# Attention scores in high and low float32r parts, with the rotated dimensions of both key segments stacked on 128 rows

## The chip, the cores and the metric

The kernel runs on one core of a Trainium2 chip. The metric is the device time of one execution in microseconds (us); the kernel before took 1618.8 us, the median of three runs (1617.66 to 1621.54). One more execution was taken with the profiler, and all rows of the trace come from it.

## The reference

The reference is a trunk of four layers on a latent sequence of 256 tokens and a context of 256 tokens, model width 1024: a gated spatial mixer (SGU), an RWKV-7 layer with a scan in both directions, a latent attention layer (MLA), and a second SGU. Only the third is touched. It projects the input to a query latent of rank 768, a key and value latent of rank 256, one shared key of 64 dimensions that is to be rotated, and gates. From the latents come 16 heads: queries of 128 unrotated ("nope") and 64 rotated ("rope") dimensions, keys of 128 nope dimensions that take the shared 64 behind them, and values of 128. Queries and keys are normalised over their 192 dimensions. Cut to what matters:

```
q_rot, k_rot = apply_rope(q, cos, sin), apply_rope(k, cos, sin)   # rotates the last 64 of 192
s = concat([q @ k_ctx.T, q_rot @ k_rot.T])                        # 256 context + 256 latent keys
p = softmax(s * 192 ** -0.5)
o = p[:, :256] @ v_ctx + p[:, 256:] @ v
x = x + gate * ((o * silu(z)) @ w_out)
```

So a query meets the context keys unrotated and the latent keys rotated.

## The kernel before, in words

All activations lie with features on the 128 partitions and tokens along the columns: 512 columns, first the context, then the latent segment (`X` is the slice of the latter). Large products are made from pieces in the type float32r: a value is cut into a high part, rounded to float32r, and a low part, the rest; hi*hi + hi*lo + lo*hi stands for the product. `split` makes both parts, the high one as a copy on ScalarE (ACT), the low one as a subtraction on VectorE (DVE). `mm3` issues the products, `wload` brings a weight tile by a DMA from SyncE's (SP's) queue and splits it (lines 178, 183, 184), with `raw`, `hi` and `lo` buffers in rings. `phase` sets the sizes of these rings: the MLA layer has four `raw` tiles of 1024 columns and three of `hi` and `lo`.

`mla` first makes the latents and the shared key `kr` (its 64 rows stand twice, on rows 0 to 63 and 64 to 127). Then 16 steps of gates (`gates`) run interleaved with `latents` and with the projection of the first pair of heads. After it comes a loop over eight pairs `g`: `attend(g)` and `project(g + 1)` are interleaved, and from `g` = 5 on some blocks of the output projection too.

`project` makes for one pair: two heads' nope keys (`keys`: product, copy, square, sum with the shared key's squares), values (`values`), and in `scaled` the key's norm `r` over 192 dimensions, the scaled nope key (L1207) and the scaled rope key, 64 rows a head, both heads in one tile `krh` (L1208). Then the rope queries of both heads together (`qo`, one head on each half of the rows), their rotated copy (`rotate`: a product with a matrix that swaps the halves of 32 with a sign on TensorE (PE), two multiplications with cosine and sine and an addition on DVE), and the nope queries (`queries`), with their norms (`norms`, which go into the softmax's scale).

`attend` makes a score block of 128 queries of one head against 512 keys in one bank of PSUM, by three products in plain float32: nope over 512 columns (L1304), unrotated rope over the 256 context columns on 64 rows (L1305), rotated rope over the 256 latent columns on 64 rows (L1306). Row maximum on DVE (L1308), exponential with a row sum on ACT (L1311), division on DVE (L1313). `weighted` transposes the block on PE, multiplies with the values, applies the gate and splits the result for the output projection; it runs one head late.

The order is set by a planner at build time: it takes the instructions in order of the program's interleaving, lets ready ones go ahead on a simulated clock, and gives each engine a fixed queue. A tile's buffers (the last number in `tl(tag, shape, bufs)`) are released when its last reader is done. On the chip each engine runs its queue in order and waits on semaphores.

Of the kernel before, what the change touches and what calls it, by code (L numbers as in the profile page):

```python
# [9 lines left out]
F32R = mybir.dt.float32r  # L10
AF = mybir.ActivationFunctionType
ALU = mybir.AluOpType
# [5 lines left out]
T = 512  # L18
# [80 lines left out]
def body(tc, I, out):  # L99
# [70 lines left out]
    def wload(src, n=None):  # L170
        return next(wparts(src, n))
# [896 lines left out]


    def mla(m):  # L1070
        with phase("2", 0, 0, 4, psum=(("pA", 4), ("pB", 4)), wn=1024, hi=3):
            ep = env["a"]

            def tl(tag, shape, bufs, dtype=F32):
# [97 lines left out]
            def rotate(dst, src):  # L1172
                p = ps("sw", "pA")
                PE.matmul(p[:, 0:256], swap, src, start=True, stop=True)
                t = tl("t1", q256, 4)
                V.tensor_tensor(t, p[:, 0:256], rope[:, 1], ALU.mult)
                V.tensor_tensor(dst, src, rope[:, 0], ALU.mult)
                V.tensor_tensor(dst, dst, t, ALU.add)

            def project(g, d):  # L1180

                w = wload(I["ml_kv"][g])
                d["kn"] = []
                kt = lambda: tl("hx" if g else "s", [128, T], 8 if g else 16)
                d["krh"], d["v"] = kt(), []

                def keys(hh):
                    p = ps("kn", "pA")
                    for k in range(2):
                        sl = slice(k * 256 + hh * 128, k * 256 + hh * 128 + 128)  # L1190
                        mm3(p, w[0][:, sl], w[1][:, sl], ckv[k], k == 0, k == 1)
                    t = kt()
                    S.copy(t, p)
                    sq = tl("lt", [128, T], 4)
                    S.activation(sq, t, AF.Square)
                    V.tensor_tensor(sq[0:64], sq[0:64], krs, ALU.add)
                    d["kn"].append(t)
                    return sq

                def scaled(hh, sq):  # L1200
                    p = ps("kss", "pA")
                    PE.matmul(p, ones, sq, start=True, stop=True)
                    hf = slice(64 * hh, 64 * hh + 64)
                    r = tl("lt", [128, T], 4)
                    rsqrt_bc(r, p, 1.0 / 192, eps)
                    t = d["kn"][hh]
                    V.scalar_tensor_tensor(out=t, in0=t, scalar=vec[:, 10:11], in1=r, op0=ALU.mult, op1=ALU.mult)  # L1207
                    V.tensor_tensor(d["krh"][hf], krg[hf], r[hf], ALU.mult)  # L1208

                def values(tb):  # L1210
                    p = ps("pv", "pA")
                    t = tl("v", [128, 2, 256], 4)
                    for b in range(2):
                        pp_ = p[:, b * 256:b * 256 + 256]
                        for k in range(2):
                            sl, ws = slice((tb + b) * 128, (tb + b) * 128 + 128), slice(512 + k * 256, 768 + k * 256)
                            PE.matmul(pp_, ckv[k][:, 0, sl], w[0][:, ws], start=k == 0, stop=False)
                            PE.matmul(pp_, ckv[k][:, 0, sl], w[1][:, ws], start=False, stop=False)
                            PE.matmul(pp_, ckv[k][:, 1, sl], w[0][:, ws], start=False, stop=k == 1)
                        d["v"].append(t[:, b])  # L1220
                    S.copy(t.rearrange("p a b -> p (a b)"), p)

                k0 = keys(0)
                yield
                k1 = keys(1)
                yield
                values(0)
                yield
                scaled(0, k0)
                yield  # L1230
                values(2)
                yield
                scaled(1, k1)
                yield
                qo, ro, qrs = tl("qo", q256, 2), tl("qr", q256, 2), tl("t1", q256, 4)
                mm256(wload(I["ml_qr"][g], 768), cq, qo)
                S.activation(qrs, qo, AF.Square)
                S.activation(qo, qo, AF.Identity, scale=vec[:, 9:10])
                yield
                d["qo"], d["qr"], d["qn"] = qo, ro, []  # L1240
                d["rq"] = rq = tl("rq", [128, 4], 2)

                def queries(hh):
                    hf = slice(64 * hh, 64 * hh + 64)
                    t = tl("qn", q256, 4)
                    mm256(wload(I["ml_qn"][g * 2 + hh], 768), cq, t)
                    sq = tl("t1", q256, 4)
                    S.activation(sq, t, AF.Square)
                    V.tensor_tensor(sq[hf], sq[hf], qrs[hf], ALU.add)
                    S.activation(t, t, AF.Identity, scale=vec[:, 8:9])  # L1250
                    d["qn"].append(t)
                    return sq

                def norms(hh, sq):
                    pq = ps("qss", "pA")
                    for qb in range(2):
                        PE.matmul(pq[:, qb:qb + 1], sq[:, qb * 128:qb * 128 + 128], ones[:, 0:1], start=True, stop=True)
                    rh = rq[:, hh * 2:hh * 2 + 2]
                    S.activation(rh, pq[:, 0:2], AF.Ln, scale=1.0 / 192, bias=eps)
                    S.activation(rh, rh, AF.Exp, scale=-0.5, bias=lsc)  # L1260

                q0 = queries(0)
                yield
                rotate(ro, qo)
                yield
                q1 = queries(1)
                norms(0, q0)
                yield
                yield
                norms(1, q1)  # L1270
                yield
# [22 lines left out]
            def attend(g, d, before):  # L1294

                rq = d["rq"]
                for hh in range(2):
                    hf = slice(64 * hh, 64 * hh + 64)
                    pt = []
                    for qb in range(2):  # L1300
                        qs = slice(qb * 128, qb * 128 + 128)
                        j = hh * 2 + qb
                        p = ps("sc", "pB")
                        PE.matmul(p, d["qn"][hh][:, qs], d["kn"][hh], start=True, stop=False)  # L1304
                        PE.matmul(p[:, 0:256], d["qo"][hf, qs], d["krh"][hf, 0:256], start=False, stop=False)  # L1305
                        PE.matmul(p[:, 256:512], d["qr"][hf, qs], d["krh"][hf, 256:512], start=False, stop=True)  # L1306
                        sm = tl("sm", [128, 4], 4)
                        V.tensor_reduce(out=sm[:, 0:1], in_=p, op=ALU.max, axis=AX.X)  # L1308
                        V.scalar_tensor_tensor(out=sm[:, 1:2], in0=sm[:, 0:1], scalar=-1.0, in1=rq[:, j:j + 1], op0=ALU.mult, op1=ALU.mult)
# [14 lines left out]
            cq = [tl("cq", [128, 2, 256], 6, F32R) for _ in range(6)]  # L1324
            ckv = [tl("ckv", [128, 2, T], 2, F32R) for _ in range(2)]
            krs = tl("krs", [64, T], 1)
            krg = tl("krg", [128, T], 1)

            def latents():
                yield from latent(ckvr, 6, 256, T, ckv)  # L1330
                S.activation(krs, kr[0:64], AF.Square)
                S.activation(krg, kr, AF.Identity, scale=vec[:, 11:12])
                krr = tl("t1", q256, 4)
                rotate(krr, krg[:, X])
                V.tensor_copy(krg[:, X], krr)
                yield
                yield from latent(cqr, 0, 768, 256, cq)

# [66 lines left out]
```

## Time and profile before

| what | value |
|---|---|
| median of three runs | 1618.8 us |
| the profiled execution | 1616.74 us |
| its span, first to last instruction | 1615.0 us |
| mean granted clock of TensorE, share of full | 0.970 |
| attention layer, from the latents to the last score | about 1046 to 1385 us |
| of it the loop over head pairs | about 1152 to 1390 us |
| period of the loop while it is regular | 28.53 us |

Busy times are unions of an engine's instructions, without issuing or waiting. Matmuls are pipelined and their ends are modelled, so the price of a stream of matmuls is read from their starts. In a timeline, brackets behind a row say how long the engine was idle before it and what ended that. PEld is TensorE's loading of weights, which overlaps PE.

### The profile page before, as it was taken

What the parts mean: (1) busy time and instruction counts of PE and PEld (TensorE: products, weight loads), DVE (VectorE), ACT (ScalarE), POOL (GpSimd) and SP (SyncE); (2) the same over time, 40 slices, a digit from 0 to 9 for tenths busy, and PEclk for the clock granted to TensorE, in tenths of its full rate; (3) what the DMA queues carried; (4) which work ended last, traced back from release to release, by engine and by line L of the source; (5) the groups of instructions that cost most, each with busy time, mean ns of one, the idle gap of its engine ahead of it and who ended that gap; (6) DMA issues with size and microseconds to landing.
All of it is one profiled execution on the core that took longest, in us unless ns stands there. A gap on an engine that the chain in (4) does not pass through costs nothing.

```text
span 1615.0 us, 28890 instructions
## 1 busy us (share of the span) xinstructions
PE 1516.5 (94%) x11666; PEld 1173.8 (73%) x11666; DVE 1151.3 (71%) x2101; ACT 788.0 (49%) x1404; POOL 124.8 (8%) x156
## 2 busy tenths in 40 slices
PE   5999999999599998899899899899999999979998
PEld 2787888888467644777676677678777777768887
DVE  3789998845788367586796854778766666665876
ACT  4544231222455353444445333569866766456543
POOL 0000000000500142212303000000000000000000
PEclk8999999999799999799999999999999999989999
DMA  9676658631044553432433133134321232265452
GB/s 366 242 288 232 234 192 305 233 105 52 36 145 167 174 159 77 145 90 80 126 103 87 59 113 103 62 129 137 121 76 47 78 92 92 66 234 196 169 183 79
DMA packets 95174, 229.05 MB, mean 142 GB/s; under 512 B 26048, under 2 KB 52160, under 8 KB 80576
## 3 DMA queue, kind: packets, MB, share of 16 engines
q1 hardware_dynamic: 92736, 223.00, 41.1%
q10 hardware_dynamic: 2304, 4.20, 0.7%
q8 instruction: 92, 1.51, 0.4%
q14 instruction: 42, 0.34, 0.1%
HBM read 208.81 MB, written 17.83 MB: 140 GB/s over the span
## 4 chain that ended last, share of the span: by engine, by line
PE 46%; DVE 6%; ACT 6%; issue 1%; POOL 1%; DMA 0%; ACTq 0%; DVEq 0%; POOLq 0%
PE fm L310 4%; PE op L310 4%; PE pg L904 3%; PE op L975 2%; PE fm L311 2%; PE op L311 2%; PE pz L310 2%; PE pu L310 2%; PE po L1286 2%; PE sc L1304 2%; PE pe L790 2%; PE sc L1305 1%; PE pv L376 1%; PE pz L311 1%; PE pv L377 1%
## 5 line engine op out<-in xcount | busy, mean ns | idle before, releaser
L184 DVE TENSOR_TENSOR lo<-raw,hi 128x2048 fp32r<-128x2048 f32 (+3 forms) x147 | 247.2, 1683 | 105.0 <-ACT hi L183 104.4
L183 ACT CAST hi<-raw 128x2048 fp32r<-128x2048 f32 (+3 forms) x161 | 212.3, 1324 | 218.8 <-PE op L314 40.5
L251 DVE SCALAR_TENSOR_TENSOR junk<-adaw,scb 128x1024 f32<-128x1024 f32 x112 | 136.9, 1222 | 13.6 <-DMA adaw<-in_ada_wT 11.7
L310 PE MATMUL op<-s,hi 128*128 128x512 f32 x256 | 91.6, 400 | 0.0
L375 PE MATMUL pv<-hi,hp 128*128 128x512 f32 x192 | 76.6, 401 | 9.1 <-ACT hi L183 6.0
L376 PE MATMUL pv<-lo,hp 128*128 128x512 f32 x192 | 76.4, 398 | 1.7 <-DVE lo L184 1.7
L310 PE MATMUL fm<-hx,hi 128*128 128x512 f32 x200 | 73.8, 409 | 4.1 <-ACT hx L304 3.8
L377 PE MATMUL pv<-hi,hp 128*128 128x512 f32 x192 | 76.2, 397 | 0.0
L904 PE MATMUL pg<-xz,wz 128*128 128x256 f32 x256 | 71.1, 412 | 0.0
L311 PE MATMUL op<-s,lo 128*128 128x256 f32 x256 | 71.1, 280 | 0.0
L313 PE MATMUL pj<-xs,hi 128*128 128x512 f32 x128 | 53.9, 423 | 12.3 <-ACT xs L304 10.2
L794 DVE TENSOR_TENSOR E<-pe,masks 128x512 f32<-128x512 f32 x64 | 41.6, 683 | 26.6 <-PE pe L790 23.9
L695 POOL TENSOR_TENSOR BK<-f 64x256 f32<-64x256 f32 x64 | 56.5, 882 | 44.3 <-DVE f L688 31.2
L311 PE MATMUL fm<-hx,lo 128*128 128x256 f32 x200 | 56.5, 287 | 2.0 <-DVE lo L184 2.0
L1004 PE MATMUL pv<-wv,xv 128*128 128x512 f32 x128 | 57.3, 596 | 0.0
L310 PEld LDWEIGHTS op<-s,hi 128*128 128x128 f32 x256 | 48.1, 188 | 12.6 <-issue 1.3
L314 PE MATMUL pj<-xs,hi 128*128 128x512 f32 x128 | 52.7, 412 | 4.0 <-DVE xs L305 4.0
L310 PE MATMUL fm<-cq,hi 128*128 128x512 f32 x144 | 55.7, 423 | 0.0
L904 PEld LDWEIGHTS pg<-xz,wz 128*128 128x128 f32 x256 | 47.1, 197 | 11.5 <-issue 3.6
L975 PE MATMUL op<-Y,wo 128*128 128x256 f32 x192 | 53.8, 415 | 1.3 <-DVE xT L979 1.3
L315 PE MATMUL pj<-xs,lo 128*128 128x512 f32 x128 | 52.5, 412 | 2.2 <-DVE lo L184 2.1
L313 PE MATMUL pu<-hp,hi 128*128 128x512 f32 x128 | 50.7, 396 | 0.0
(392 smaller groups left out, 4027.3 us busy)
## 6 DMA issues: line engine op xcount, KB each, us to landing
adaw<-in_ada_wT SPq DMA_DIRECT2D x36, 1024.0 KB, 6.2
raw<-in_sgu_v SPq DMA_DIRECT2D x16, 1024.0 KB, 5.9
raw<-in_sgu_u SPq DMA_DIRECT2D x16, 1024.0 KB, 5.3
raw<-in_sgu_z SPq DMA_DIRECT2D x16, 1024.0 KB, 5.0
raw<-in_sgu_o SPq DMA_DIRECT2D x16, 1024.0 KB, 4.8
adaw<-in_ada_w SPq DMA_DIRECT2D x24, 512.0 KB, 10.2
xz<-xz SPq DMA_DIRECT2D x32, 256.0 KB, 3.9
raw<-in_ml_z SPq DMA_DIRECT2D x16, 512.0 KB, 3.7
```

The lines of the kernel that those rows point to most:

```text
L183: S.copy(hi[:, sl], raw[:, sl])
L184: (nc.gpsimd if parts > 1 and i else V).tensor_tensor(lo[:, sl], raw[:, sl], hi[:, sl], ALU.subtract)
L251: V.scalar_tensor_tensor(out=junk, in0=raw[:, f, :], scalar=1.0, in1=scb[:, c, :], op0=ALU.mult, op1=ALU.mult, accum_out=m[:, t * 2 + f, c ...
L310: PE.matmul(p, whi, x, start=start, stop=False)
L311: PE.matmul(p[:, 0:256], wlo, x[:, 0], start=False, stop=stop)
L313: PE.matmul(p, whi, x[:, 0], start=start, stop=False)
L375: PE.matmul(pv[tb], hs[k][:, 0, sl], whi[:, ws_], start=k == 0, stop=False)
L376: PE.matmul(pv[tb], hs[k][:, 0, sl], wlo[:, ws_], start=False, stop=False)
L377: PE.matmul(pv[tb], hs[k][:, 1, sl], whi[:, ws_], start=False, stop=k == 7)
L904: PE.matmul(p, ws[k // 4][:, k % 4, pr * 128:pr * 128 + 128], xs[k // 2][:, k % 2, :], start=k == 0, stop=k == 7)
L975: PE.matmul(p[:, ob], w[:, k, ob, :], y[:, k], start=k == 0, stop=k == 1)
L1004: PE.matmul(p, xv[:, k, tb * 128:tb * 128 + 128], ws[k // 4][:, k % 4, :], start=k == 0, stop=k == 7)
```

## The change

Four things. (1) The nope keys and nope queries are kept as high and low parts (`kt` tiles in float32r; `qn` with two halves), and a nope score is three float32r products. (2) The rope part of both segments becomes one product over 128 rows: the queries of a head hold the unrotated 64 dimensions on one half of the rows and the rotated ones on the other (`qo`, one column block a head); the keys `krg[hh]` hold the unrotated shared key in the context columns of the first half, the rotated one in the latent columns of the other half, and zeros elsewhere. This product is split too, so a score block is six float32r products of 512 columns. (3) For that, the rope queries are scaled into the two halves by two ACT instructions, copied to the opposite rows by two DMAs on SP's queue (`qx`), rotated from there, and added into place by two 64-row additions; the scaled rope keys are made by a multiplication on GpSimd (POOL) and split by ACT and DVE. (4) `raw` has three buffers, not four; `hx` tiles are taken four a pair, not three; `qo` and `qx` have one buffer each, `qn` three, the stacked and split keys (`rp`) three, the stacked and split queries (`qp`) two.

```diff
@@ -1068,7 +1068,7 @@
 
 
     def mla(m):
-        with phase("2", 0, 0, 4, psum=(("pA", 4), ("pB", 4)), wn=1024, hi=3):
+        with phase("2", 0, 0, 3, psum=(("pA", 4), ("pB", 4)), wn=1024, hi=3):
             ep = env["a"]
 
             def tl(tag, shape, bufs, dtype=F32):
@@ -1174,38 +1174,44 @@
                 PE.matmul(p[:, 0:256], swap, src, start=True, stop=True)
                 t = tl("t1", q256, 4)
                 V.tensor_tensor(t, p[:, 0:256], rope[:, 1], ALU.mult)
-                V.tensor_tensor(dst, src, rope[:, 0], ALU.mult)
-                V.tensor_tensor(dst, dst, t, ALU.add)
+                u = tl("t1", q256, 4)
+                V.tensor_tensor(u, src, rope[:, 0], ALU.mult)
+                for hf, x in dst:
+                    V.tensor_tensor(x, u[hf], t[hf], ALU.add)
 
             def project(g, d):
 
                 w = wload(I["ml_kv"][g])
                 d["kn"] = []
-                kt = lambda: tl("hx" if g else "s", [128, T], 8 if g else 16)
-                d["krh"], d["v"] = kt(), []
+                kt = lambda: tl("hx" if g else "s", [128, T], 8 if g else 16, F32R)
+                d["kr"], d["v"] = [], []
 
                 def keys(hh):
                     p = ps("kn", "pA")
                     for k in range(2):
                         sl = slice(k * 256 + hh * 128, k * 256 + hh * 128 + 128)
                         mm3(p, w[0][:, sl], w[1][:, sl], ckv[k], k == 0, k == 1)
-                    t = kt()
+                    t = tl("kf", [128, T], 2)
                     S.copy(t, p)
                     sq = tl("lt", [128, T], 4)
                     S.activation(sq, t, AF.Square)
                     V.tensor_tensor(sq[0:64], sq[0:64], krs, ALU.add)
-                    d["kn"].append(t)
-                    return sq
-
-                def scaled(hh, sq):
+                    return t, sq
+
+                def scaled(hh, t, sq):
                     p = ps("kss", "pA")
                     PE.matmul(p, ones, sq, start=True, stop=True)
-                    hf = slice(64 * hh, 64 * hh + 64)
                     r = tl("lt", [128, T], 4)
                     rsqrt_bc(r, p, 1.0 / 192, eps)
-                    t = d["kn"][hh]
                     V.scalar_tensor_tensor(out=t, in0=t, scalar=vec[:, 10:11], in1=r, op0=ALU.mult, op1=ALU.mult)
-                    V.tensor_tensor(d["krh"][hf], krg[hf], r[hf], ALU.mult)
+                    x = kt(), kt()
+                    S.copy(x[0], t)
+                    V.tensor_tensor(x[1], t, x[0], ALU.subtract)
+                    d["kn"].append(x)
+                    nc.gpsimd.tensor_tensor(r, krg[hh], r, ALU.mult)
+                    x = tl("rp", [128, 2, T], 3, F32R)
+                    split(r, x)
+                    d["kr"].append(x)
 
                 def values(tb):
                     p = ps("pv", "pA")
@@ -1226,29 +1232,36 @@
                 yield
                 values(0)
                 yield
-                scaled(0, k0)
+                scaled(0, *k0)
                 yield
                 values(2)
                 yield
-                scaled(1, k1)
-                yield
-                qo, ro, qrs = tl("qo", q256, 2), tl("qr", q256, 2), tl("t1", q256, 4)
-                mm256(wload(I["ml_qr"][g], 768), cq, qo)
-                S.activation(qrs, qo, AF.Square)
-                S.activation(qo, qo, AF.Identity, scale=vec[:, 9:10])
-                yield
-                d["qo"], d["qr"], d["qn"] = qo, ro, []
+                scaled(1, *k1)
+                yield
+
+                qo, qx, qrs = tl("qo", [128, 2, 256], 1), tl("qx", q256, 1), tl("t1", q256, 4)
+                qt = tl("t1", q256, 4)
+                mm256(wload(I["ml_qr"][g], 768), cq, qt)
+                S.activation(qrs, qt, AF.Square)
+                for hh in range(2):
+                    hf, of = (slice(64 * i, 64 * i + 64) for i in (hh, 1 - hh))
+                    S.activation(qo[hf, hh], qt[hf], AF.Identity, scale=vec[hf, 9:10])
+                    nc.sync.dma_start(out=qx[of], in_=qo[hf, hh])
+                yield
+                d["qn"] = []
                 d["rq"] = rq = tl("rq", [128, 4], 2)
 
                 def queries(hh):
                     hf = slice(64 * hh, 64 * hh + 64)
-                    t = tl("qn", q256, 4)
+                    t = tl("qf", q256, 2)
                     mm256(wload(I["ml_qn"][g * 2 + hh], 768), cq, t)
                     sq = tl("t1", q256, 4)
                     S.activation(sq, t, AF.Square)
                     V.tensor_tensor(sq[hf], sq[hf], qrs[hf], ALU.add)
-                    S.activation(t, t, AF.Identity, scale=vec[:, 8:9])
-                    d["qn"].append(t)
+                    x = tl("qn", [128, 2, 256], 3, F32R)
+                    S.activation(x[:, 0], t, AF.Identity, scale=vec[:, 8:9])
+                    V.scalar_tensor_tensor(out=x[:, 1], in0=t, scalar=vec[:, 8:9], in1=x[:, 0], op0=ALU.mult, op1=ALU.subtract)
+                    d["qn"].append(x)
                     return sq
 
                 def norms(hh, sq):
@@ -1261,7 +1274,9 @@
 
                 q0 = queries(0)
                 yield
-                rotate(ro, qo)
+                rotate([(slice(64, 128), qo[64:128, 0]), (slice(0, 64), qo[0:64, 1])], qx)
+                d["qr"] = tl("qp", [128, 2, 2, 256], 2, F32R)
+                split(qo, d["qr"])
                 yield
                 q1 = queries(1)
                 norms(0, q0)
@@ -1295,15 +1310,16 @@
 
                 rq = d["rq"]
                 for hh in range(2):
-                    hf = slice(64 * hh, 64 * hh + 64)
                     pt = []
                     for qb in range(2):
                         qs = slice(qb * 128, qb * 128 + 128)
                         j = hh * 2 + qb
                         p = ps("sc", "pB")
-                        PE.matmul(p, d["qn"][hh][:, qs], d["kn"][hh], start=True, stop=False)
-                        PE.matmul(p[:, 0:256], d["qo"][hf, qs], d["krh"][hf, 0:256], start=False, stop=False)
-                        PE.matmul(p[:, 256:512], d["qr"][hf, qs], d["krh"][hf, 256:512], start=False, stop=True)
+                        (kh, kl), q = d["kn"][hh], d["qn"][hh]
+                        PE.matmul(p, q[:, 0, qs], kh, start=True, stop=False)
+                        PE.matmul(p, q[:, 0, qs], kl, start=False, stop=False)
+                        PE.matmul(p, q[:, 1, qs], kh, start=False, stop=False)
+                        mm3(p, d["qr"][:, 0, hh, qs], d["qr"][:, 1, hh, qs], d["kr"][hh], False, True)
                         sm = tl("sm", [128, 4], 4)
                         V.tensor_reduce(out=sm[:, 0:1], in_=p, op=ALU.max, axis=AX.X)
                         V.scalar_tensor_tensor(out=sm[:, 1:2], in0=sm[:, 0:1], scalar=-1.0, in1=rq[:, j:j + 1], op0=ALU.mult, op1=ALU.mult)
@@ -1324,15 +1340,20 @@
             cq = [tl("cq", [128, 2, 256], 6, F32R) for _ in range(6)]
             ckv = [tl("ckv", [128, 2, T], 2, F32R) for _ in range(2)]
             krs = tl("krs", [64, T], 1)
-            krg = tl("krg", [128, T], 1)
+
+
+            krg = [tl(f"krg{hh}", [128, T], 1) for hh in range(2)]
 
             def latents():
                 yield from latent(ckvr, 6, 256, T, ckv)
                 S.activation(krs, kr[0:64], AF.Square)
-                S.activation(krg, kr, AF.Identity, scale=vec[:, 11:12])
-                krr = tl("t1", q256, 4)
-                rotate(krr, krg[:, X])
-                V.tensor_copy(krg[:, X], krr)
+                S.activation(kr, kr, AF.Identity, scale=vec[:, 11:12])
+                for hh in range(2):
+                    hf, of = (slice(64 * i, 64 * i + 64) for i in (hh, 1 - hh))
+                    nc.gpsimd.memset(krg[hh][hf, X], 0.0)
+                    nc.gpsimd.memset(krg[hh][of, 0:256], 0.0)
+                    S.copy(krg[hh][hf, 0:256], kr[hf, 0:256])
+                rotate([(slice(64, 128), krg[0][64:128, X]), (slice(0, 64), krg[1][0:64, X])], kr[:, X])
                 yield
                 yield from latent(cqr, 0, 768, 256, cq)
 
```

## Rows read from the trace of the kernel before

**Rows 1.** The page: busy us (share of the span) and instructions of each engine
```profile
PE 1516.5 (94%) x11666; PEld 1173.8 (73%) x11666; DVE 1151.3 (71%) x2101; ACT 788.0 (49%) x1404; POOL 124.8 (8%) x156
```

**Rows 2.** Busy by window: length, PE, PEld, DVE, ACT, POOL, granted clock, DMA
```profile
1092.00:1152.00 60.00, 58.29 (x326) 49.53 (x325) 51.66 (x97) 56.70 (x128) 0.00 (x0) 1.00 0.48 149
1192.92:1221.45 28.53, 28.53 (x144) 21.39 (x143) 18.18 (x39) 19.59 (x43) 0.00 (x0) 1.00 0.20 60
```

**Rows 3.** Timeline of PE at a score block: start, duration, line, operation
```profile
1195.43 1.02 PE L1304 MATMUL sc<-hx,qn 128*128 128x512 f32 x2
...
1197.44 0.50 PE L310 MATMUL fm<-cq,hi 128*128 128x512 f32 x1
```

**Rows 4.** Timeline of PE in a key projection, inside the loop
```profile
1180.88 0.39 PE L315 MATMUL kn<-ckv,lo 128*128 128x512 f32 x1
...
1181.57 0.40 PE L315 MATMUL kn<-ckv,lo 128*128 128x512 f32 x1
1181.90 0.48 PE L1306 MATMUL sc<-hx,qr 64*128 64x256 f32 x1
```

**Rows 5.** Groups by line, 1080:1390 us: count, busy us, mean ns, idle before
```profile
L1308 DVE TENSOR_REDUCE sm<-sc 128x1 f32<-128x512 f32 x32 | 22.0, 686 | 10.7 <-PE sc L1306 10.7
L304 ACT CAST ckv<-s 128x512 fp32r<-128x512 f32 x2 | 1.2, 620 | 0.0
L304 ACT CAST cq<-v 128x256 fp32r<-128x256 f32 x6 | 2.5, 409 | 0.0
L305 DVE TENSOR_TENSOR ckv<-s,ckv 128x512 fp32r<-128x512 f32 x2 | 1.4, 688 | 0.0
L1238 ACT ACTIVATE qo<-qo,vec 128x256 f32<-128x256 f32 x8 | 4.1, 510 | 0.2
L1249 DVE TENSOR_TENSOR t<-t,t 64x256 f32<-64x256 f32 x16 | 6.7, 417 | 0.7 <-ACT t L1248 0.2
L1208 DVE TENSOR_TENSOR hx<-krg,lt 64x512 f32<-64x512 f32 x14 | 9.6, 683 | 0.1
```

**Rows 6.** Groups of POOL by line; then a timeline in an earlier layer
```profile
L493 POOL TENSOR_TENSOR xx<-hp 128x512 f32<-128x512 f32 x7 | 10.1, 1438 | 2.3 <-DVE xs L499 1.9 <-ACT hp L491 0.4
...
424.44 2.31 POOL L184 TENSOR_TENSOR lo<-raw,hi 128x256 fp32r<-128x256 f32 x2
424.95 1.21 DVE L305 TENSOR_TENSOR xs<-xs 128x512 fp32r<-128x512 f32 x1
```

**Rows 7.** Timeline: the rotation's chain and its reader in one period
```profile
1198.63 0.51 ACT L1238 ACTIVATE qo<-qo,vec 128x256 f32<-128x256 f32 x1
1202.85 0.41 DVE L1178 TENSOR_TENSOR qr<-qr,t 128x256 f32<-128x256 f32 x1
1203.07 1.02 PE L1304 MATMUL sc<-hx,qn 128*128 128x512 f32 x2
1204.89 0.59 PE L1306 MATMUL sc<-hx,qr 64*128 64x256 f32 x2
```

**Rows 8.** DMA issues: count, KB each, median us from issue to landing
```profile
UV<-vt SPq DMA_DIRECT2D x64, 64.0 KB, 2.7
vt<-v SPq DMA_DIRECT2D x32, 64.0 KB, 1.8
raw<-in_ml_qn SPq DMA_DIRECT2D x16, 384.0 KB, 3.1
```

**Rows 9.** Timeline of SP's queue: weight loads in one period
```profile
1192.79 0.33 SPq L178 DMA_DIRECT2D raw<-in_ml_qn  x1
1204.99 0.33 SPq L178 DMA_DIRECT2D raw<-in_ml_qn  x1
```

**Rows 10.** Waits, 1092:1152 us: us in total, times, longest us
```profile
PEld fm L311 <- DVE lo L184: 2.5, 2, 1.3
PE fm L311 <- DVE lo L184: 1.7, 2, 1.0
```

**Rows 11.** Timeline of PE where the next layer begins
```profile
1421.14 1.22 PE L375 MATMUL pv<-hi,hp 128*128 128x512 f32 x2 [6.02 <-ACT hi L183]
```

## The prediction

> **What bounds the kernel now.** I read the page's busy times first [rows 1]: TensorE (PE) is busy 94% of the span, VectorE (DVE) 71%, ScalarE (ACT) 49%. That is a mean over four layers, so the next view is the busy time by window for the attention layer, the only one that the diff touches [rows 2]. There the reader is to see two regimes. From 1092 to 1152 us the gates and the projections of the first head pair run: ACT is busy 56.70 of 60 us and PE 58.29, so both are nearly full. From about 1152 the loop over eight head pairs runs; one period of it, 1192.92 to 1221.45 us, has PE busy 28.53 of 28.53 us, ACT 19.59 and DVE 18.18. PE is the bound of the loop, with no hole, and ACT and DVE have about 9 us of slack per period. A busy PE need not be a PE at its peak, so I then read the starts of its matmuls one by one [rows 3]: one score block (a 128-query block of one head) begins at 1195.43 and the next work at 1197.44. It holds PE for 2.01 us, four of these in a period.
>
> **Part 1, the scores (removed and added on PE).** Before, a block is one 512-column and two 256-column products in float32, each run as two passes, the last two on 64 rows. After, it is six 512-column float32r products with all 128 rows: three for the unrotated part, three for the stacked rotated part. The price of one such product stands in the key projection [rows 4]: three starts on, from 1180.88 to 1181.57, are 0.69 us, that is 0.23 us each. Six are 1.38 to 1.40 us. The saving is 2.01 - 1.40 = 0.61 us a block; there are 32 blocks (32 row maxima [rows 5]), so 19.5 us, all on the bound engine: a period falls from 28.53 to 26.1 us of PE work. The zeros in the keys cost nothing by themselves, since rows are free and columns are what is paid. The swap product of the rotation stays as it is.
>
> **Part 2, what ACT and DVE get instead** [rows 5]. Per head pair ACT gains four 128x512 copies (high parts of two nope keys and of two stacked rope keys) and one more for the stacked queries, 5 x 0.62 = 3.1 us, and the scaling of the rope queries becomes two 64-row ones, which by columns cost 0.51 us each instead of one: together +3.6. DVE gains five 128x512 subtractions, 5 x 0.69 = 3.4, one more 64x256 addition and two more 128x256 operations, 3 x 0.42 = 1.3, and loses two 64x512 multiplications, 2 x 0.68 = 1.4: together +3.3. In a loop period that makes ACT 23.2 and DVE 21.5 us beside 26.1 of PE. PE remains the longest, so none of this is paid directly; but the cover shrinks from 9 us to 3 or 4, and this is where I expect some of the saving to be given back.
>
> **Part 3, the multiplication moved to GpSimd (POOL).** Two 128x512 products per pair; the nearest row has 1.44 us for one [rows 6]. POOL is idle in this layer. It is not free for DVE: in an earlier stage a DVE product with two SBUF inputs that meets POOL work took 1.21 us [rows 6] where the same shape alone takes 0.69 [rows 5]. Two POOL operations a period, meeting one DVE operation each, are 2 x 0.52 = 1.0 us; bounds 0 (no meeting) and 2 x 1.44 = 2.9. I take 1.0: DVE becomes 22.5 of 26.1, still covered. The Trainium skill, in "SBUF — State Buffer", section "Who interferes with whom", says that a DVE instruction with two SBUF inputs contends with a GpSimd instruction that reads SBUF, and that whoever is late for the shared pair blocks fully. By that, DVE would stand for up to the whole POOL operation; the row shows a wait of a part of one, and either leaves DVE below PE here.
>
> **Part 4, the DMAs in the rotation's chain.** Before, the rotated queries are ready when L1178 ends, 1202.85 + 0.41 = 1203.26, and PE reads them at 1204.89 [rows 7]: 1.6 us to spare. The new chain has, behind the scaling that began at 1198.63: another 0.51 of scaling, a 64 KB transfer (1.8 to 2.7 us for that size [rows 8], between DRAM and SBUF; SBUF to SBUF is not in the trace), 0.41 for a second addition, and the split, 0.62 + 0.69. That is 4.0 to 4.9 us more. And PE asks earlier: its first read of the stacked queries follows three products, 0.7 us, instead of the 1204.89 - 1203.07 = 1.8 us of before. So the data come 4.0 + 1.1 - 1.6 = 3.5 to 4.4 us late against an unchanged order. What is queued behind the waiting product on PE: the rest of the score, then transposes and value products of the pair before, and everything else, in order. Whether PE stands depends on what the planner puts ahead of it. Fillers exist: early in the loop the key products of the next pair were put ahead of the rotated part of a score that was late [rows 4], six of them, 1.4 us by their price, and there are two heads to a pair. Bounds of the loss per period: 0 (all filled) and 3.5 us (nothing filled, low end of the lateness). Nearest to the row with fillers, but with ACT and DVE now at 86 to 89%, I take 1.0 us for all waits of PE in a period, DVE's meeting POOL included: 7 periods with a projection in them, 7.0 us.
>
> The transfers go on SP's queue, which also brings the weights. Behind a transfer that waits for ACT stand weight loads. One raw buffer less means that a load goes out three casts ahead: 1192.79 to 1204.99, 12.2 us, at the tightest [rows 9], against 3.1 us to land [rows 8]. The 9 us between hide the wait; without them every late load would stop PE for its lateness.
>
> **Part 5, the stage before the loop.** The first pair's projection lies under the gates, where ACT has only 3.3 us left of 60 and PE already waited 2.5 + 1.7 us for split weights [rows 2, 10]. ACT gets +3.6, and for the shared keys two copies of 64x256 more, at most 2 x 0.41 by the 128x256 cast [rows 5]: 4.4 us. Nothing covers it fully; some can slide past 1152. Bounds 0 and 4.4, taken 2.5. The four memsets go to an idle POOL and are off the path.
>
> **Part 6, the ends of the layer.** The tiles take more room and the weight buffers less, so the places that the next layer's first weights wait for move. There PE stands 6.02 us for a split weight [rows 11]. I take 0, with 3 us to either side (half of that wait), because nothing in the trace tells which way.
>
> **Sum.** -19.5 + 7.0 + 2.5 + 0 = -10.0 us. The profiled execution took 1616.74 us (span 1615.0 and 1.7 around it), 2.1 below the median 1618.8 of the runs shown: 1606.7 by its own time, 1608.8 against the median. I predict 1609.
>
> **The rivals.**
> A. PE alone counts: the planner fills every wait, the loop keeps no hole. For: in the period before there is none [rows 2]. Against: then it had 9 us of cover. Time: 1618.8 - 19.5 + 2.5 = 1602, down to 1598 with the low ends.
> B. The gain is given back: waits of 2 to 3 us in each period. For: in the gates' stage, with ACT at 94%, PE lost 4.2 us of 60, 7%, which on 26 us is 1.8. Against: the loop's ACT would be at 89%. At 2.4 us a period the time is 1618.8 - 19.5 + 2.5 + 7 x 2.4 = 1618.6.
> C. Slower: the transfer stands in PE's way in every period. PE waits the 3.5 us of part 4, ACT's full 4.4 us come on top: -19.5 + 24.5 + 4.4 = +9.4, 1628. It decides from a wait of 2.4 us a period (the saving left after the gates' stage, 17, over 7). For: single buffers for the stacked queries and their swapped copy. Against: the fillers.
> D. That a float32r product of 512 columns takes longer in a score than in the key projection: I see no reason, the rows are of the same shape, and give it no chance of its own.
>
> **How the numbers follow.** A change of 0.3%, 4.9 us, is about what can be told from none. The forecast (0.4 to 1.7 us lost a period, 1604 to 1614) gets 0.45, A 0.20, B 0.19 (1614 to 1624), C 0.16. The likeliest case's own range is 1603 to 1614. To hold 8 in 10 the range takes in A and most of B: 1599 to 1622. Faster by over 0.3% (below 1613.9): nearly all of the forecast and A, 0.65; within 0.3%: B, 0.19; slower: C, 0.16.
>
> **What would show it.** Part 1: starts of 0.23 us apart in the score lines, a block of 1.4 us. Part 2: ACT near 23 and DVE near 22 us in a period, and a period near 27. Part 3: two-input DVE operations of about 1.2 us beside POOL. Part 4: whether the waits of PE name the swap product or the first product with the stacked queries, and how long. Part 5: the stage of the gates longer by 2 to 3 us. The prediction is wrong if the period is above 28.5 us, if PE's clock falls from its full level, which the loop now holds [rows 2], or if the layers around move by more than 3 us.

## The result: slower by 0.8%, and the profile after

The changed kernel took 1632.2 us (median of six runs, 1627.8 to 1633.7) beside 1618.8 us of the kernel before (six runs, 1613.8 to 1621.5): a ratio of 1.0082, 95% interval 1.0063 to 1.0102. The forecast was 1609, its range 1599 to 1622. Rival C, with 1628, came nearest. The profiled execution took 1631.08 us, its span 1629.3 us, 14.3 more than before.

The page's busy times, beside [rows 1]:

```profile
PE 1504.5 (92%) x11666; PEld 1184.6 (73%) x11666; DVE 1185.7 (73%) x2149; ACT 811.2 (50%) x1454; POOL 148.0 (9%) x176
```

PE is busy for 12 us less and the span is 14 us longer, so PE now stands. To see where, I cut the layer at three instructions that both kernels have: the layer's first norm product, the first score product, and the last one. First the kernel before, then the one after; columns as in [rows 2] (length, PE, PEld, DVE, ACT, POOL, granted clock, DMA).

```profile
1045.85:1152.24 106.39, 100.22 (x538) 83.97 (x539) 85.43 (x167) 85.53 (x184) 0.00 (x0) 0.95 0.45 143
1152.24:1384.39 232.15, 232.15 (x1160) 174.13 (x1158) 151.14 (x307) 153.65 (x312) 0.00 (x0) 1.00 0.25 77
```

```profile
1046.83:1158.99 112.16, 101.84 (x538) 85.26 (x539) 89.87 (x170) 89.29 (x192) 2.59 (x2) 0.94 0.44 138
1158.99:1398.06 239.07, 219.68 (x1160) 183.84 (x1158) 181.09 (x350) 172.65 (x353) 18.10 (x14) 0.96 0.26 78
```

The first line of each is the stage ahead of the loop, the second the loop. The loop was full of PE work at a granted clock of 1.00, its upper level (2.4 GHz); now it holds 219.68 us of PE work and 19.4 us in which PE stands, at a mean clock of 0.96. Below, a loop with the same products at 1.00 holds 213.03 us of PE work (the third line of experiment 1), so 6.7 of the 219.68 are the clock. The loop's account is then: 232.15 - 19.1 (scores) + 6.7 (clock) + 19.4 (waits) = 239.1. With +5.8 in the stage ahead, +1.0 ahead of the layer and +0.6 behind the last score, that is 14.3.

A period of the regular part, from one issue of the rotation's transfer to the next, beside the period of [rows 2] (the one ahead of it, from 1206.27, is as long), then a short window behind its wait; and the waits of PE in the loop (what waits, on what, us in total, times, longest):

```profile
1237.23:1268.18 30.95, 27.57 (x142) 23.03 (x142) 22.77 (x45) 22.55 (x47) 2.57 (x2) 0.94 0.20 60
...
1241.40:1243.50 2.10, 2.10 (x8) 1.81 (x8) 1.54 (x5) 0.76 (x3) 0.00 (x0) 0.50 0.08 25
```

```profile
PE sw L1174 <- DMA qx<-qo: 10.2, 3, 3.4
PE po L1301 <- ACT pT L1297: 5.9, 3, 2.1
PE sw L1174 <- ACT t L1259: 3.4, 1, 3.4
```

A period of 30.95 us is 3.4 us of standing and 27.6 of work; the same 142 products take 26.4 us in a period at 1.00 (the second line of experiment 1). Four waits of 3.4 us, 13.6 of the 19.4, are at one instruction, the rotation's swap product (L1174). All four are for the transfer: each product starts 2.66 to 2.67 us after the first of its two transfers was issued, also the one for which the view names an ACT instruction (1299.11 to 1301.77). Its timeline (start, duration, line, operation; in brackets the idle time before it):

```profile
1239.89 0.67 PE L1174 MATMUL sw<-qx,swap 128*128 128x256 f32 x2 [3.37 <-DMA qx<-qo]
1240.21 0.58 PE L310 MATMUL fm<-cq,hi 128*128 128x512 f32 x1
...
1242.00 0.63 PE L310 MATMUL fm<-cq,hi 128*128 128x512 f32 x1
...
1242.64 0.63 PE L310 MATMUL fm<-cq,hi 128*128 128x512 f32 x1
```

Right behind it stands a projection of ready data (the next queries) that could have filled the wait, but the queue is in order. And behind the wait the granted clock fell: it is 0.50, the lower level (1.2 GHz), from 1241.40 to 1243.50, and there a pair of products takes 0.64 us (starts at 1242.00 and 1242.64). In experiment 2 the same pairs start 0.35 us apart (1262.54 to 1262.89) in a period at 1.00.

The chain that feeds the swap product, one period on; its product starts at about 1270.8, PE's last product ahead of it (the score) began at 1267.07. Rows of four engines in order of time, others left out:

```profile
1263.39 1.29 POOL L1211 TENSOR_TENSOR lt<-krg,lt 128x512 f32<-128x512 f32 x1 [5.61 <-DVE kf L1206]
1263.44 2.33 DVE L184 TENSOR_TENSOR lo<-raw,hi 128x1024 fp32r<-128x1024 f32 x1 [0.19 <-ACT hi L183]
1264.72 0.62 ACT L304 CAST rp<-lt 128x512 fp32r<-128x512 f32 x1 [0.80 <-POOL lt L1211]
1265.25 0.36 ACT L1112 COPY t<-fm 128x256 f32<-128x256 f32 x1
1265.70 0.68 DVE L1209 TENSOR_TENSOR hx<-kf,hx 128x512 fp32r<-128x512 f32 x1
1266.30 0.68 DVE L305 TENSOR_TENSOR rp<-lt,rp 128x512 fp32r<-128x512 f32 x1
1266.90 0.41 DVE L1113 TENSOR_TENSOR t<-t,fm 128x256 f32<-128x256 f32 x1
1267.34 0.42 ACT L1245 ACTIVATE t<-t 128x256 f32<-128x256 f32 x1 [0.99 <-DVE t L1113]
1267.66 1.02 ACT L1248 ACTIVATE qo<-t,vec 64x256 f32<-64x256 f32 x2
1268.18 0.47 SPq L1249 DMA_DIRECT2D qx<-qo  x1
```

Read it backwards. The transfers are issued from 1268.18 (64 KB, a median of 2.0 us from issue to landing); ACT scales from 1267.66; the raw rope queries are complete at 1266.90 + 0.41 on DVE; and DVE comes to them late, because two new subtractions (L1209, L305) stand ahead of it and because L184, which began 0.05 us after POOL's product, took 2.33 us. In experiment 5, without POOL work here, it takes 1.22. L1113's own operand is late too: ACT copies it out of PSUM (L1112) only at 1265.25, behind the new casts (L1208 and L304), and had stood 0.80 us for POOL's product ahead of the second.

The other three waits, 1.6 to 2.1 us each, are at a value product (L1301) that needs ACT's copy of the transposed scores. In two of them ACT had stood 1.46 us for the same L1113 and then had the scalings of the rope queries ahead of that copy. In the third (1179.29) ACT stood only 0.21 us, for POOL, and the casts and scalings were ahead of the copy. One of the two:

```profile
1370.25 0.42 ACT L1245 ACTIVATE t<-t 128x256 f32<-128x256 f32 x1 [1.46 <-DVE t L1113]
1370.57 1.02 ACT L1248 ACTIVATE qo<-t,vec 64x256 f32<-64x256 f32 x2
1372.64 1.08 ACT L1297 COPY pT<-pT 128x512 f32<-128x512 f32 x2
1373.78 1.15 PE L1301 MATMUL po<-pT,v 128*128 128x256 f32 x2 [2.12 <-ACT pT L1297]
```

### The profile page after: what moved, and what is told of

It reads as the page before. It is cut to its first block, busy times and chain, and to the rows that moved or that the text cites. A ratio compares the mean times of both kernels' runs of the same rounds, so it can differ in the third digit from the quotient of the medians.

```text
span 1629.3 us, 29051 instructions
## 1 busy us (share of the span) xinstructions
PE 1504.5 (92%) x11666; PEld 1184.6 (73%) x11666; DVE 1185.7 (73%) x2149; ACT 811.2 (50%) x1454; POOL 148.0 (9%) x176
## 4 chain that ended last, share of the span: by engine, by line
PE 39%; ACT 10%; DVE 9%; issue 2%; POOL 1%; DMA 1%; SPq 0%; ACTq 0%; POOLq 0%; DVEq 0%
PE op L310 4%; PE pg L904 3%; PE fm L310 3%; PE op L975 2%; PE op L311 2%; PE pz L310 2%; PE pu L310 2%; PE pe L790 2%; ACT hi L183 2%; PE po L1301 1%; DVE lo L184 1%; PE fm L311 1%; PE pv L376 1%; PE pv L377 1%; PE pz L311 1%
## 5 line engine op out<-in xcount | busy, mean ns | idle before, releaser
L184 DVE TENSOR_TENSOR lo<-raw,hi 128x2048 fp32r<-128x2048 f32 (+3 forms) x147 | 255.4, 1738 | 99.7 <-ACT hi L183 98.9
L310 PE MATMUL fm<-cq,hi 128*128 128x512 f32 x144 | 60.6, 452 | 0.0
```

The lines of the kernel that those rows point to most:

```text
L184: (nc.gpsimd if parts > 1 and i else V).tensor_tensor(lo[:, sl], raw[:, sl], hi[:, sl], ALU.subtract)
L310: PE.matmul(p, whi, x, start=start, stop=False)
```

## The experiments

Every kernel was timed beside the kernel before on the same chip. The total also holds the untouched layers: this layer began between 1042 and 1052 us in the profiled executions, so with each stands its loop, cut as above. The planner ordered every kernel anew, so what an edit does to the order is part of its result. The fences hold window rows (columns as in [rows 2]), then rows of the waits of PE in the loop, and timeline rows or groups by line where the text speaks of them. Theories: W, the wait of PE at the swap product, with its causes; against it, the other rows of the sum (scores not cheaper, the stage ahead, more work on ACT and DVE).

**1. Without the move of rows.** The rope queries are scaled as a whole into `qx`; this leaves out the move to the opposite rows, so the rotated part is the other head's.

```diff
-                    nc.sync.dma_start(out=qx[of], in_=qo[hf, hh])
+                S.activation(qx, qt, AF.Identity, scale=vec[:, 9:10])   # after the loop over hh
```

> The two transfers of the scaled rope queries to the other half of the rows are left out; ACT writes a copy on the same rows instead (one 128x256 operation more), and the rotation reads that, so the rotated part of each head is the other head's. Everything else of the change stays. Theory W (the wait for the transfer and TensorE's clock after it): the 3.4 to 3.5 us for which PE stands at the swap product lose the transfer's 2 us, the clock stays at its upper level, and a loop period goes from 30.95 to 26.5 to 28 us; time 1602 to 1615. Rival L (the added ACT, DVE and POOL work stretches the period, and the swap product is only where it shows): PE waits elsewhere, the period stays above 29.5 us, time 1622 to 1632.

Measured: 1611.7 us, ratio 0.9967 (0.9949 to 0.9985). The stage ahead, a regular period, the loop, and the wait:

```profile
1042.14:1150.65 108.51, 100.35 (x538) 83.93 (x539) 87.36 (x167) 88.31 (x190) 2.59 (x2) 0.96 0.43 138
1199.60:1227.73 28.13, 26.37 (x142) 21.87 (x142) 22.32 (x45) 22.59 (x49) 2.57 (x2) 1.00 0.21 61
1150.65:1375.51 224.86, 213.03 (x1159) 177.78 (x1158) 182.77 (x353) 174.69 (x363) 19.84 (x14) 1.00 0.26 81
...
PE sw L1174 <- ACT qx L1249: 10.2, 7, 1.8
```

The time is in W's range, the period just above it (28.13 us). The chain through the transfers is worth 14 us of loop, and with it gone the clock holds. But PE still stands at the same place, now for ACT: seven waits of at most 1.8 us. The transfer is about half of the lateness, not all of it; of what is left, 0.51 us is the ACT copy that replaces it.

**2. The swap product later.** The transfers stay; the rotation goes behind the next queries and the first norms, so that the ready projection is ahead of it.

```diff
                 q0 = queries(0)
                 yield
+                q1 = queries(1)
+                norms(0, q0)
+                yield
                 rotate([(slice(64, 128), qo[64:128, 0]), (slice(0, 64), qo[0:64, 1])], qx)
...
                 yield
-                q1 = queries(1)
-                norms(0, q0)
-                yield
```

> The change with one step moved in the program's order: the rotation and split of the rope queries come after the second head's query product instead of before it (some 2.1 us of PE work more between the transfer and the swap product). The same instructions. Theory W: the wait at the swap product falls below 1.5 us and the clock stays up; period 26.5 to 28 us, time 1602 to 1615. Rival L: the work is the same, so the period stays above 29.5 us, time 1622 to 1634.

Measured: 1619.8 us, ratio 1.0012 (0.9991 to 1.0033): by the ratios 11 us better than the change, between the ranges of W and L.

```profile
1268.57:1298.54 29.97, 27.95 (x144) 22.87 (x142) 22.60 (x45) 22.61 (x48) 2.57 (x2) 0.94 0.24 71
1152.13:1388.94 236.81, 225.38 (x1195) 188.84 (x1196) 185.84 (x364) 175.67 (x366) 18.87 (x14) 0.97 0.27 83
...
PE qss L1270 <- DVE t L1260: 11.3, 7, 2.0
...
1267.79 0.61 PE L1270 MATMUL qss<-ones,t 128*128 128x1 f32 x4 [1.74 <-DVE t L1260]
1268.57 0.59 PE L1174 MATMUL sw<-qx,swap 128*128 128x256 f32 x2
```

The swap product no longer waits. The norms' small products (L1270), now ahead of it, wait up to 2.0 us for DVE. So the wait moved to the next instruction that needs the late DVE: the lateness of DVE, with ACT ahead of it, is a cause of its own. The first line is a period whose only wait is one of 2.0 us there; its clock is 0.94.

**3. Work put into the wait.** Six products of 64 rows on old data, into the unused half of the swap product's bank.

```diff
                 p = ps("sw", "pA")
+                for _ in range(0 if fill is None else 6):
+                    PE.matmul(p[:, 256:512], swap[0:64], fill, start=True, stop=True)
```

> The change with six useless swap products (64 rows, 256 columns, float32, about 0.43 us each) ahead of each rope query's swap product; they read the first scaled half, which is there before the transfer lands, and write unused columns. Theory W: the wait is filled with work, so the clock stays up and the products behind it run at full speed: about 1.9 us less in each of the periods in which it fell, 1618 to 1627 in all, though 2.6 us of work were added to PE per pair. Rival L, and the wait alone without the clock: not faster than the changed kernel, 1630 to 1640.

Measured: 1638.4 us, ratio 1.0133 (1.0103 to 1.0164). W's total was missed by 11 us; the time lies in L's range.

```profile
1205.10:1235.35 30.25, 28.82 (x154) 24.00 (x154) 22.52 (x45) 22.16 (x48) 2.57 (x2) 1.00 0.20 61
1265.57:1299.05 33.48, 32.28 (x155) 26.42 (x156) 22.70 (x45) 22.53 (x48) 2.57 (x2) 0.90 0.20 63
1156.05:1401.46 245.41, 237.47 (x1243) 198.01 (x1242) 181.55 (x350) 172.18 (x356) 18.03 (x14) 0.97 0.24 76
...
PE sw L1175 <- ACT qo L1250: 7.6, 7, 1.4
...
1265.57 4.34 PE L1175 MATMUL sw<-qo,swap 64*128 64x256 f32 x12 [1.43 <-ACT qo L1250]
```

In the first regular period the wait falls to 1.4 us, the clock holds 1.00, and the period is shorter by 0.7 us than the change's although 2.6 us of products were put in: that much fits W. A later period has a clock of 0.90: there the fillers themselves, behind 1.43 us of standing, took 4.34 us. And over the loop the fillers' 7 x 2.6 = 18 us exceed the waits that they replace. So this does not show what makes the clock fall: less standing did not keep it up everywhere.

**4. The first part alone.** On the kernel before, only the nope keys and queries become high and low parts; the rope stays as before, `raw` has three buffers.

```diff
-                        PE.matmul(p, d["qn"][hh][:, qs], d["kn"][hh], start=True, stop=False)
+                        (kh, kl), q = d["kn"][hh], d["qn"][hh]
+                        PE.matmul(p, q[:, 0, qs], kh, start=True, stop=False)
+                        PE.matmul(p, q[:, 0, qs], kl, start=False, stop=False)
+                        PE.matmul(p, q[:, 1, qs], kh, start=False, stop=False)
```

> The first part of the change alone, on the kernel before: nope scores as three float32r products of high and low parts; the rope scores stay two 64-row float32 products of 256 columns, no transfers, no POOL work, no zeros; three raw weight buffers as in the change. By the stride of 0.23 us a score block is 0.70 + 1.06 = 1.76 us on PE instead of 2.01: 8 us less in all. ACT gains 1.2, DVE 1.4 + 0.9 us per pair. Theory W: nothing waits for a transfer, so 1610 to 1616. Rival L: the added work stretches the period by itself, 1619 to 1628.

Measured: 1612.6 us, ratio 0.9971 (0.9954 to 0.9987).

```profile
1044.01:1150.35 106.34, 100.17 (x539) 84.24 (x539) 86.30 (x168) 85.26 (x184) 0.00 (x0) 0.95 0.45 142
1150.35:1378.58 228.23, 228.18 (x1190) 179.66 (x1189) 162.61 (x336) 158.42 (x327) 0.00 (x0) 1.00 0.25 79
```

The cheaper product pays without any wait, but half of what was expected: PE has 4.0 us less work in the loop (232.15 to 228.18), not 8. In its trace, the first of the three products starts 0.42 us ahead of the second where a float32 product stands before it (1203.96 to 1204.38), and the third 0.32 us ahead of the float32 product behind it (1206.46 to 1206.78), instead of 0.23; in the whole change all six are of one type. And the stage ahead is as long as before (106.34 beside 106.39), so the third `raw` buffer cost nothing there. The loss of the change is in its rope half.

**5. The rope keys' product on DVE.** The change, with one word different.

```diff
-                    nc.gpsimd.tensor_tensor(r, krg[hh], r, ALU.mult)
+                    V.tensor_tensor(r, krg[hh], r, ALU.mult)
```

> The change with the multiplication of the rope keys by their norm on DVE instead of POOL; all else, the transfers too, stays. Theory P (POOL's reads hold up DVE on the chain to the swap product: the 128x1024 subtraction there took 2.33 us instead of 1.23): DVE gets 0.69 us more of work per operation, but loses the 1.1 us of holding up; the scaled queries come up to 1 us earlier, PE's wait at the swap product falls from 3.54 to 2.5 to 3.2 us, and where the clock then stays up the period goes from 30.95 to 28.7 to 29.5 us; time 1612 to 1626. Rival (contention does not matter, the transfer alone does): wait 3.4 to 3.6 us or more, time 1630 to 1637.

Measured: 1620.1 us, ratio 1.0008 (0.9987 to 1.0028).

```profile
1157.82:1386.72 228.90, 216.79 (x1160) 181.44 (x1158) 177.13 (x363) 171.00 (x354) 0.00 (x0) 0.98 0.27 81
...
PE po L1301 <- ACT pT L1297: 6.1, 4, 2.1
PE sw L1174 <- ACT t L1259: 5.8, 3, 2.1
...
L184 DVE TENSOR_TENSOR lo<-raw,hi 128x1024 fp32r<-128x1024 f32 x16 | 19.5, 1220 | 3.0 <-ACT hi L183 3.0
```

Twelve us by putting more work on DVE: the same subtraction takes 1220 ns on average in the loop, beside 1491 in the change; L1209's takes 686 beside 940. The waits at the swap product, still for the transfer (issued at 1259.28, product at 1261.93), fall from 13.6 to 5.8 us; those at the value product stay. DVE's busy time in the loop falls too (181.1 to 177.1), though it does 13 operations more.

**6. No transfers.** The swap matrix is built so that it crosses the two halves of rows, and a second product brings the unswapped copy across; the rest moves on ACT and POOL.

```diff
+    o["swap"] = np.concatenate([np.kron(np.eye(2, dtype=f)[::-1], b) for b in (sw, np.eye(64, dtype=f))], 1)
...
+                for i in range(2):
+                    PE.matmul(p[:, i * 256:i * 256 + 256], swap[:, i * 128:i * 128 + 128], src, start=True, stop=True)
...
+                V.tensor_tensor(u, p[:, 256:512], rope[:, 0], ALU.mult)
...
+                S.activation(qx, qt, AF.Identity, scale=vec[:, 9:10])
...
+                    nc.gpsimd.tensor_copy(qo[hf, hh], qx[hf])
```

> The change without transfers, with the same results: two swap products on PE, with matrices that also move the rows to the other half (one rotates, one copies), from one scaled 128x256 tile; POOL copies the scaled halves into place; the unsplit nope queries have one buffer. PE pays one more 256-column product, 0.43 us a pair. Theory W: no wait for a transfer and no fall of the clock; what stays is the wait on ACT and DVE, 1.9 us where the move was only left out, 1.0 to 1.9 here; a period of 27.6 to 28.6 us, time 1605 to 1615. Rival L: above 1618.

Measured: 1610.9 us, ratio 0.9943 (0.9923 to 0.9963). The clock holds; 8.1 us of waits at the swap product are left, for ACT.

```profile
1151.89:1378.33 226.44, 218.20 (x1189) 183.15 (x1189) 184.70 (x359) 171.56 (x356) 25.52 (x28) 1.00 0.26 81
...
PE sw L1175 <- ACT qx L1247: 8.1, 7, 1.4
```

**7. Both, 5 and 6 together.**

> As the kernel with two swap products, and the multiplication of the rope keys by their norm on DVE instead of POOL. Theory P: the wait of PE at the swap product falls by another 0.4 to 1.1 us a pair; period 26.8 to 27.8 us, time 1600 to 1610. Rival: DVE has 1.4 us more to do and the wait stays or grows; 1610 to 1618.

Measured: 1602.2 us, ratio 0.9899 (0.9863 to 0.9935), and once more below: 1607.0 us, 0.9926 (0.9900 to 0.9951).

> The kernel with two swap products and the multiplication on DVE once more, beside the one with the late rotation on the same chip: 1600 to 1606, a period of 26.9 us as before.

```profile
1153.67:1369.62 215.95, 215.85 (x1174) 180.15 (x1172) 177.15 (x365) 167.41 (x348) 9.17 (x14) 1.00 0.27 84
...
1225.09:1251.97 26.88, 26.88 (x145) 22.07 (x144) 21.85 (x47) 21.53 (x47) 1.14 (x2) 1.00 0.22 64
```

The loop has no hole, as before the change, and is 16.2 us shorter than then. It repeats: 215.88 us in the second profile. The second median, 4.7 us higher, is just above the 1606 expected, and the difference is not in the loop: in the two profiled executions the layer began at 1044.8 and at 1050.6 us. Both intervals lie below 1, so this version is faster than the kernel before, and than the changed one.

**8. Transfers kept, 2 and 5 together.**

> The change with its transfers kept, but both other edits together: the rotation behind the second head's query product, and the rope keys' multiplication on DVE instead of POOL. If a transfer costs PE only through the place of its reader and the lateness of the chain ahead of it, not through being a transfer: no wait over 1 us in the regular periods, the clock up, a period of 26.5 to 27.5 us, time 1600 to 1609, like the kernel without transfers. If a transfer in the chain costs by itself: a period above 28 us, time 1612 to 1620.

Measured: 1608.7 us, ratio 0.9929 (0.9905 to 0.9953).

```profile
1236.16:1262.66 26.50, 26.00 (x144) 21.82 (x144) 21.65 (x47) 22.06 (x47) 0.00 (x0) 1.00 0.24 70
1155.29:1376.91 221.62, 218.16 (x1196) 184.14 (x1196) 181.29 (x378) 175.37 (x366) 0.00 (x0) 1.00 0.30 89
...
PE qss L1270 <- DVE t L1260: 3.5, 6, 0.7
```

With its reader placed later and DVE not held up, the transfers stay and no wait of PE names the swap product: in the loop 3.5 us are left for DVE, and 2.1 for ACT ahead of its first score. This order moves a projection of the first pair from the stage ahead into the loop, so the two are taken together: 325.2 us beside 324.8 in experiment 7, 338.5 before and 351.2 in the change. Experiment 7 waits for nothing in the loop, but with its second swap products PE has 317.9 us of work in the two, beside 312.6 here.

## Why the prediction was wrong, point by point

**The step that failed** is in part 4: "Nearest to the row with fillers [...], I take 1.0 us for all waits of PE in a period". PE stood 3.4 us in each regular period, 19.4 in the loop where 7.0 were priced. The lateness itself had been worked out as 3.5 to 4.4 us; what was wrong was to let the queue absorb it. I argued that fillers exist, and they do (the next queries' projection is the very next thing on PE), but no row said that they would be put ahead of a late instruction: the score of [rows 4] that I called late was not late on the chip. The rotated queries of that stretch were complete on DVE at 1175.41 us, and PE read them at 1181.90. Nor did the late reader turn out to be the one I named, the first product with the stacked queries: PE met the lateness one step earlier, at the swap product, where only the transfer and not the second addition and the split had passed.

So it is luck that 3.4 lies next to the 3.5 worked out for another place. At the swap product that working has 0.51 of scaling and 1.8 to 2.7 of transfer, less the 0.94 us by which its operand was early before (complete at 1198.63 + 0.51, [rows 7]):

```profile
1200.08 0.60 PE L1174 MATMUL sw<-qo,swap 128*128 128x256 f32 x2
```

That is 1.4 to 2.3 us. The rest of the wait is the lateness of the raw queries on ACT and DVE, which parts 2 and 3 had set aside as covered. Experiment 8 shows that the same transfers, with DVE not held up and under another order, cause no wait of PE. Why the planner's simulated clock put the swap product there stays open.

**TensorE's clock** was named as what would make the prediction wrong, and given no price and no chance. It cost 6.7 us of the loop. It fell in the regular periods with 3.4 us of standing and stayed at 1.00 in experiment 1 with waits of up to 1.8; but it fell to a mean of 0.94 in a period of experiment 2 with 2.0 us and to 0.90 in one of experiment 3 behind 1.4, so what decides it stays open.

**Part 1** held. Three of the six products of a score block:

```profile
1266.37 0.39 PE L1321 MATMUL sc<-hx,qn 128*128 128x512 f32 x1
1266.60 0.40 PE L313 MATMUL sc<-rp,qp 128*128 128x512 f32 x1
1266.84 0.40 PE L314 MATMUL sc<-rp,qp 128*128 128x512 f32 x1
```

Starts are 0.23 to 0.24 us apart, as in [rows 4] (0.32 behind the first, 1265.81 to 1266.13, which follows the transposes); with experiment 1's loop, 232.15 - 213.03 = 19.1 us against the 19.5 forecast. Rival D is out.

**Part 2** held as a sum: ACT 22.5 (23.2 forecast) and DVE 22.8 us in a period (21.5 plus 1.0 for POOL). The inference did not: "none of this is paid directly" compares totals over a period, but what PE waits for is one chain, and the new operations of both engines stood ahead of L1113 on it.

**Part 3** was off in size and in place. One meeting cost 2.33 - 1.22 = 1.1 us, not the 0.52 of [rows 6], where DVE came 0.5 us into a POOL operation of about 1.16 (2.31 us for two), and it fell on the chain to the swap product, where slack on average is no help. The Trainium skill, "SBUF — State Buffer", section "Who interferes with whom", says that the one that comes late blocks fully; the trace agrees closely (DVE lost 1.1 of the 1.24 us that POOL's operation still ran), and the prediction had cited this and set it aside as hidden. Experiment 5 prices the move to POOL at 12 us, hold-up and POOL's longer product (1.29 us against the 0.68 of a DVE product of that shape, [rows 5]) together.

**Part 5** had 2.5 for the stage ahead; it grew by 5.8. The rest is again the swap product: PE waits 3.5 us there for the first pair. In experiment 1, where that wait is 1.4, the stage is 2.1 us longer than before; in 7, without it, 2.5.

**Part 6** held within its 3 us: +0.6 behind the last score. SP's weight loads, which part 4 called hidden, name no wait of PE in the loop.

**The rivals.** C was the right mechanism and nearly the right price (3.5 us a period), at 0.16. That its total came so near is partly luck: it has seven waits of 3.5 us, 24.5, where the loop has 19.4 of waits and 6.7 of clock. It had only the transfer in it; the runs show two causes: without the transfers 22 us are won, without POOL 12, without both 25 to 30 (by ratios against the kernel before: 1.0082 to 0.9943, 1.0008, and 0.9899 or 0.9926). A is about what both repairs give. B's price rests on a double count, which part 5 has too: [rows 10] shows the same two waits once at the weight load and once at the product, and PE was idle for 60 - 58.29 = 1.7 us there, not 4.2.

## What to carry to other kernels

When an engine runs its queue in order, slack counted by busy time says nothing about a late operand: follow the chain of each instruction on the bounding engine to the place where that engine reads it, and price the whole lateness unless a row shows what stands ahead of it. Put a transfer between a producer and the bounding engine only with ready work ahead of its reader, and don't move a product to POOL beside a chain of two-input operations on DVE that is nearly due. A wait on TensorE can cost more than itself, so give a fall of its clock a price when a new wait of some us is possible.

## What was not expected of the hardware

- A DVE subtraction of 128x1024 with both inputs in SBUF took 2.33 us where it met a POOL product of 1.29 us at its start, and 1.22 us where there was none; giving DVE that product as well made DVE's busy time shorter.
- Behind a wait of 3.4 us the granted clock fell, and the period's work took 27.6 us where the same products take 26.4 at 1.00: 1.2 us, about a third of the wait once more.
- 64 KB from SBUF to SBUF took 2.0 us from issue to landing, within the bounds taken from transfers with DRAM [rows 8].
